# One core, a hybrid state-space and attention trunk: state-space tensors regrouped by chunk through DRAM, softmax tiles copied per query tile, one Gelu

## The chip, the cores and the metric

One NeuronCore of a Trainium2 chip runs the whole program. The metric is device time in microseconds (us) of one execution. The engines are TensorE (PE in the rows, with PEld for its weight loads), VectorE (DVE), ScalarE (ACT), GpSimd (POOL) and SyncE (SP), which here issues nearly every DMA, from one queue and in a fixed order.

## The reference, cut to what matters

One layer, sequence of 512 positions, model width 2048, everything in float32.

```
proj = h @ w_in            # u | conv | q k v | indexer
# (A) S5 state space, 512 channels in 32 groups of 16, then Gelu and a GLU
y = Re(C x) + d * u,  x[t] = lam_bar * x[t-1] + B_bar u[t]
g = gelu(y);  y_ssm = g * sigmoid(g @ w_glu + b_glu)
# (B) gated short convolution
# (C) 8 heads of 128: keys chosen by an indexer (top-k), then
s = softmax(q k^T * scale, masked to the chosen keys);  y_attn = s v
y = concat(rms(y_ssm), rms(y_conv), rms(y_attn)) @ w_o     # then LayerNorm
out = LayerNorm(alpha * x + gate * (relu(h2 @ w_ff1)^2 @ w_ff2))
```

## The kernel before, in words

One function, `trunk_kernel`, is written with a tile framework. Each engine runs one static list of instructions; the framework sets that list from the order of the code and from priorities (`with prio("ssm")`: each block has an offset in a table). Blocks of higher priority run where their data allow; the large float32 matmuls of the projections, which are split in two halves each (`wh`, `wl`), fill the rest of TensorE. Tensors lie transposed, channels on the partitions.

The program runs in stages. From 0 to about 235 us come the conditioning vector and the first input projections, among them `u_t` (128 x 4 x 512: the 512 state-space channels over time). From about 235 to 445 us come the rotary embedding of q and k (`cos_t`, `sin_t`, L401 to L419, with `sw` as its scratch tile), the indexer and the top-k, which are VectorE work, over the projection of k on TensorE. From about 440 to 710 us the projections of v (`wv`, evacuated from PSUM by ACT copies into `ve`) and of the convolution (`wconv`) fill TensorE, and the state space and the attention are woven into them. Then come the GLU, the output projection (`wo`), LayerNorm and the two feed-forward products, up to the end.

The state space goes in four rounds m of 128 channels. `ssm_in` (L674) loads `bc`, builds small matrices on DVE, and regroups `u_t[:, m]` from channels x time into `uc`, in which a partition holds one of four places in a chunk and 32 channels: 16 ACT copies of 32 x 128 elements. `ssm_scan` (L711) multiplies (L716) and runs the recurrence on DVE. `ssm_direct` (L736) prepares the matrices of the direct part. `ssm_out` (L773) does the output matmuls (L777 to L779) into a PSUM bank (`sb`), copies them back to channels x time with another 16 ACT copies of 32 x 128, into a tile that is also called `uc`, adds `d * u` on DVE and applies Gelu on ACT. The GLU (L800) loads its weights `wg` and multiplies (L807).

The attention goes by head h and query tile t. `att_scores` (L858): one score matmul (L863) into one of two PSUM banks named `sa`, mask and minimum on DVE (L866), exponential on ACT, reciprocal on DVE, scaling on ACT (`s`). `att_turn` (L873): t+1 transposes (L876) into an `sa` bank, and t+1 ACT copies of 128 x 128 into the tiles `pt0` to `pt3`, one for each tile of keys. `att_values` (L880): four matmuls (L884), 512, 384, 256 and 128 columns wide, into an `sa` bank, an ACT copy into `qh`, and a write to `y_d`. Both banks of `sa` are shared by scores, transposes and values, so a late ACT copy out of one holds the next of them.

Every ACT copy goes through a helper and has the line L57; most DVE operations have L60 or L63.

Of the kernel before, what the change touches and what calls it, by code (L numbers as in the profile page):

```python
# [51 lines left out]
def trunk_kernel(ctx, tc, A, out):  # L52
    nc = tc.nc
    V, S, G, T = nc.vector, nc.scalar, nc.gpsimd, nc.tensor

    def act(o, i, f=AF.Copy, **kw):
        S.activation(o, i, f, **kw)  # L57
# [4 lines left out]
    def stt(o, a, s, b, op0, op1):  # L62
        V.scalar_tensor_tensor(o, a, s, b, op0=op0, op1=op1)  # L63
# [17 lines left out]
    def prio(name):  # L81
        if name not in PRIO:
            name += str(stage_no[0])
        return tc.high_priority(offset=PRIO[name])
# [14 lines left out]
    def col(n, i=0, w=1):  # L99
        o = COLS[n][0]  # L100
        return cols[:, o + i:o + i + w]
# [306 lines left out]
    nc.sync.dma_start(cos_t, A["rope_q"][0])  # L408
    nc.sync.dma_start(sin_t, A["rope_q"][1])

    def rope_t(dst, src):

        sw = TB.tile([128, SEQ], F32, name="sw", bufs=2)
        act(sw[0:64], src[64:128])
        act(sw[64:128], src[0:64])
        tt(dst, src, cos_t, OP.mult)
        tt(sw, sw, sin_t, OP.mult)
        tt(dst, dst, sw, OP.add)
# [257 lines left out]
    def ssm_in(m):  # L676

        p4 = slice(4 * m, 4 * m + 4)

        def pb(x, s):  # L680
            return x[:, p4, 0:s, None].to_broadcast([128, 4, s, 16])

        bc = SP.tile([128, 4, 4, 16], F32, name="bc")
        nc.sync.dma_start(bc, A["ssm_bc"][:, :, p4])
        uc = SP.tile([128, 4, 128], F32, name="uc", bufs=2)
        uv = u_t[:, m].rearrange("p (c s) -> p s c", s=4)
        for s in range(4):
            for p in range(4):
                act(uc[32 * s:32 * s + 32, p], uv[32 * p:32 * p + 32, s])
        tmp = SP.tile([128, 2, 4, 5, 16], F32, name="tmp")  # L690
        bb = SP.tile([128, 2, 4, 16], F32, name="bb")
        f_b = tuple(f[:, p4, None].to_broadcast([128, 4, 16]) for f in (fr, fi))
        cmul((bb[:, 0], bb[:, 1]), f_b, (bc[:, 0], bc[:, 1]), (tmp[:, 0, :, 0], tmp[:, 1, :, 0]))
        bt = SP.tile([128, 2, 4, 128], F32, name="s4", bufs=2)
        G.memset(bt, 0.0)
        ta, tb_ = tmp[:, 0, :, 0:4], tmp[:, 1, :, 0:4]
        tt(ta, pb(pwr[:, 0], 4), vb(bb[:, 0], 4), OP.mult)
        tt(tb_, pb(pwr[:, 1], 4), vb(bb[:, 1], 4), OP.mult)
        outer(bt[:, 0], ta, tb_, 4, OP.subtract)
        tt(ta, pb(pwr[:, 0], 4), vb(bb[:, 1], 4), OP.mult)  # L700
        tt(tb_, pb(pwr[:, 1], 4), vb(bb[:, 0], 4), OP.mult)
        outer(bt[:, 1], ta, tb_, 4, OP.add)
        bl = SP.tile([128, 2, 4, 128], F32, name="s4", bufs=2)
        for ri in range(2):
            ps = bank("sb")
            for p in range(4):
                T.transpose(ps[:, p * 128:(p + 1) * 128], bt[:, ri, p], ident)
            act(bl[:, ri].rearrange("p a b -> p (a b)"), ps)
        return p4, bc, bb, bl, uc
# [63 lines left out]
    def ssm_out(m, uc, x):  # L773
        ps = bank("sb")
        for p in range(4):
            o = ps[:, p * 128:(p + 1) * 128]
            T.matmul(o, toep[:, p], uc[:, p], start=True, stop=False)  # L777
            T.matmul(o[:, 1:128], cl[:, 0, p, 32:160], x[:, 0, p, 0:127], start=False, stop=False)
            T.matmul(o[:, 1:128], cl[:, 1, p, 32:160], x[:, 1, p, 0:127], start=False, stop=True)  # L779
        yt = SP.tile([128, SEQ], F32, name="uc", bufs=2)  # L780
        yv = yt.rearrange("p (c s) -> p s c", s=4)
        for t in range(4):
            for p in range(4):
                act(yv[32 * p:32 * p + 32, t], ps[32 * t:32 * t + 32, p * 128:(p + 1) * 128])
        stt(u_t[:, m], u_t[:, m], col("d", m), yt, OP.mult, OP.add)
        act(u_t[:, m], u_t[:, m], AF.Gelu_apprx_tanh)

    with prio("ssm"):
        s_in = ssm_in(0)
        for m in range(4):  # L790
            x = ssm_scan(*s_in)
            p4, bc, bb, bl, uc = s_in
            ssm_direct(p4, bc, bb)
            if m < 3:
                s_in = ssm_in(m + 1)
            ssm_out(m, uc, x)
    ssm.close()
    glu = ExitStack()
    GL = glu.enter_context(tc.tile_pool(name="glu", bufs=1, reuse_waits="tile", side="right"))
    with prio("glu"):  # L800
        wg = GL.tile([128, 4, 512], F32, name="wg")
        nc.sync.dma_start(wg, A["wglu"])
        sig = GL.tile([128, 4, SEQ], F32, name="sig")
        for m in range(4):
            ps = bank("sb")
            for k in range(4):
                T.matmul(ps, wg[:, k, m * 128:(m + 1) * 128], u_t[:, k], start=(k == 0), stop=(k == 3))  # L807
            act(sig[:, m], ps, AF.Sigmoid, bias=col("bglu", m))
        for m in range(4):
            tt(u_t[:, m], u_t[:, m], sig[:, m], OP.mult)  # L810

        ps = rms_rows(GL, square_sum(GL, [u_t[:, m] for m in range(4)], (1, 1)), 512, "sb")
        for m in range(4):
            stt(u_t[:, m], u_t[:, m], col("gn", m), ps, OP.mult, OP.mult)

# [31 lines left out]
    def att_load(h):  # L849
        qh = AT.tile([128, SEQ], F32, name="qh", bufs=2)  # L850
        kh = AT.tile([128, SEQ], F32, name="kh")
        vh = AT.tile([128, NT, 128], F32, name="vh")
        nc.sync.dma_start(qh, q_d[h])
        nc.sync.dma_start(kh, k_d[h])
        nc.sync.dma_start(vh, v_d[:, :, h * 128:(h + 1) * 128].rearrange("t p n -> p t n"))
        heads[h] = qh, kh, vh, [AT.tile([128, SEQ - 128 * j], F32, name=f"pt{j}") for j in range(NT)]

    def att_scores(h, t):  # L858

# [12 lines left out]
    def att_turn(h, t, s):  # L872

        pb_ = bank("sa")
        for j in range(t + 1):
            T.transpose(pb_[:, j * 128:(j + 1) * 128], s[:, j * 128:(j + 1) * 128], ident)  # L876
        for j in range(t + 1):
            act(heads[h][3][j][:, (t - j) * 128:(t - j + 1) * 128], pb_[:, j * 128:(j + 1) * 128])

    def att_values(h):  # L880
        qh, _, vh, pt = heads.pop(h)
        po = bank("sa")
        for j in range(NT):
            T.matmul(po[:, j * 128:], vh[:, j], pt[j], start=(j == 0), stop=(j == NT - 1))  # L884
        act(qh, po)
        nc.sync.dma_start(y_d[h], qh)
        if h == 0:
            act(sqa, qh, AF.Square)
        else:
            sq = AT.tile([128, SEQ], F32, name="s", bufs=3)  # L890
            act(sq, qh, AF.Square)
            tt(sqa, sqa, sq, OP.add)
# [14 lines left out]
        att_turn(*last)  # L907
        att_values(NH - 1)

    rsa = AT.tile([128, SEQ], F32, name="rsa")  # L910
    act(rsa, rms_rows(AT, sqa, 1024, "sa"))


# [700 lines left out]
```

## Time and profile before

| | |
|---|---|
| time, median of 3 runs | 2243.91 us (2243.41 to 2245.91) |
| the profiled execution | 2243.67 us, of which its span is 2241.9 us |
| instructions | 30919 |
| PE busy | 2151.6 us, 96% of the span |
| DVE busy | 1880.8 us, 84% |
| ACT busy | 1096.3 us, 49% |
| mean granted TensorE clock | 0.985 |

The profiled execution is one run on the chip with the hardware profiler; its span is from its first instruction to its last. Shares of busy time are means over stages that have different limits, so the rows further down are taken by stage. PE busy counts matmul time alone; weight loads (PEld) run beside it.

### The profile page before, as it was taken

What the parts mean: (1) busy time and instruction counts of PE and PEld (TensorE: products, weight loads), DVE (VectorE), ACT (ScalarE), POOL (GpSimd) and SP (SyncE); (2) the same over time, 40 slices, a digit from 0 to 9 for tenths busy, and PEclk for the clock granted to TensorE, in tenths of its full rate; (3) what the DMA queues carried; (4) which work ended last, traced back from release to release, by engine and by line L of the source; (5) the groups of instructions that cost most, each with busy time, mean ns of one, the idle gap of its engine ahead of it and who ended that gap; (6) DMA issues with size and microseconds to landing.
All of it is one profiled execution on the core that took longest, in us unless ns stands there. A gap on an engine that the chain in (4) does not pass through costs nothing.

```text
span 2241.9 us, 30919 instructions
## 1 busy us (share of the span) xinstructions
PE 2151.6 (96%) x11947; PEld 1848.8 (82%) x11947; DVE 1880.8 (84%) x2520; ACT 1096.3 (49%) x1570; POOL 44.6 (2%) x55
## 2 busy tenths in 40 slices
PE   6999999988899999999999999999899999999997
PEld 4778887866676787889999999999778888888886
DVE  7886889998776777698888888887689989998788
ACT  3322444467864312656656566665444444444432
POOL 0000000000000000000000000000000000000000
PEclk9999999999999999999999999999999999999999
DMA  8877554254314577656656656565788898798462
GB/s 323 320 296 275 187 196 153 104 205 138 102 66 155 197 281 285 208 191 208 208 188 203 209 181 207 179 206 166 264 284 264 313 324 267 257 347 273 129 220 85
DMA packets 192411, 485.60 MB, mean 217 GB/s; under 512 B 17412, under 2 KB 101764, under 8 KB 165896
## 3 DMA queue, kind: packets, MB, share of 16 engines
q1 hardware_dynamic: 185736, 471.04, 59.3%
q0 software_dynamic: 6528, 12.58, 3.1%
q8 instruction: 94, 1.54, 0.3%
q14 instruction: 53, 0.43, 0.1%
HBM read 392.35 MB, written 78.64 MB: 210 GB/s over the span
## 4 chain that ended last, share of the span: by engine, by line
PE 68%; DVE 20%; ACT 5%; DMA 4%; issue 3%; SPq 0%; DVEq 0%; ACTq 0%
PE mm L203 8%; PE mm L204 7%; PE mm L202 7%; PE two L1380 5%; PE two L1381 5%; PE two L1379 5%; DVE wl L60 5%; PE mm L197 4%; PE mm L198 3%; PE mm L196 3%; PE mm L210 3%; PE mm L209 3%; PE mm L208 3%; DVE ffa L60 2%; DVE adaz L63 2%
## 5 line engine op out<-in xcount | busy, mean ns | idle before, releaser
L57 ACT ACTIVATE wh<-raw 128x1024 fp32r<-128x1024 f32 x332 | 351.3, 1059 | 446.9 <-PE two L1381 141.5
L60 DVE TENSOR_TENSOR wl<-raw,wh 128x1024 fp32r<-128x1024 f32 x332 | 403.5, 1219 | 108.2 <-ACT wh L57 107.3
L1379 PE MATMUL two<-wh,hin 128*128 128x512 f32 x784 | 307.6, 392 | 5.8 <-ACT wh L57 5.1
L1380 PE MATMUL two<-wl,hin 128*128 128x512 f32 x784 | 306.4, 391 | 2.3 <-DVE wl L60 2.3
L1381 PE MATMUL two<-wh,hin 128*128 128x512 f32 x784 | 306.1, 390 | 0.0
L196 PE MATMUL mm<-acts,wh 128*128 128x512 f32 (+1 forms) x568 | 226.9, 403 | 7.2 <-ACT ve L57 3.8
L197 PE MATMUL mm<-acts,wl 128*128 128x512 f32 (+1 forms) x568 | 225.9, 398 | 0.8 <-DVE wl L60 0.7
L198 PE MATMUL mm<-acts,wh 128*128 128x512 f32 (+1 forms) x568 | 224.6, 396 | 0.0
L63 DVE SCALAR_TENSOR_TENSOR adaz<-raw,cols,adaz 128x1024 f32<-128x1024 f32 (+2 forms) x180 | 198.1, 1111 | 16.2 <-DMA raw<-in_adaR_dram 10.9
L202 PE MATMUL mm<-acts,wh 128*128 128x256 f32 x720 | 204.7, 284 | 3.5 <-ACT wh L57 2.4
L203 PE MATMUL mm<-acts,wl 128*128 128x256 f32 x720 | 204.5, 284 | 1.7 <-DVE wl L60 1.7
L203 PE MATMUL mm<-tx,wl 128*128 128x256 f32 x720 | 203.8, 283 | 1.1 <-DVE wl L60 1.1
L204 PE MATMUL mm<-acts,wh 128*128 128x256 f32 x720 | 204.4, 284 | 0.0
L204 PE MATMUL mm<-tx,wh 128*128 128x256 f32 x720 | 203.4, 282 | 0.0
L202 PE MATMUL mm<-tx,wh 128*128 128x256 f32 x720 | 202.0, 281 | 0.1
L1379 PEld LDWEIGHTS two<-wh,hin 128*128 128x128 f32 x784 | 147.8, 189 | 38.3 <-ACT wh L57 6.3
L1380 PEld LDWEIGHTS two<-wl,hin 128*128 128x128 f32 x784 | 147.8, 188 | 35.1 <-DVE wl L60 4.0
L209 PE MATMUL mm<-wl,acts 128*128 128x512 f32 x448 | 175.0, 391 | 1.2 <-DVE wl L60 1.0
L210 PE MATMUL mm<-wh,acts 128*128 128x512 f32 x448 | 174.7, 390 | 0.0
L208 PE MATMUL mm<-wh,acts 128*128 128x512 f32 x448 | 173.7, 391 | 0.2 <-DVE r L60 0.2
L1381 PEld LDWEIGHTS two<-wh,hin 128*128 128x128 f32 x784 | 147.6, 188 | 30.9
L57 ACT ACTIVATE wh<-st 128x1024 fp32r<-128x1024 f32 x90 | 95.4, 1060 | 105.5 <-PE mm L204 83.9
(316 smaller groups left out, 4581.1 us busy)
## 6 DMA issues: line engine op xcount, KB each, us to landing
raw<-in_wff_dram SPq DMA_DIRECT2D x232, 512.0 KB, 4.6
hc_d<-hc SPq DMA_DIRECT2D x98, 512.0 KB, 5.0
hin<-hc_d SPq DMA_DIRECT2D x49, 1024.0 KB, 8.6
raw<-in_adaR_dram SPq DMA_DIRECT2D x48, 1024.0 KB, 5.2
raw<-in_adaS_dram SPq DMA_DIRECT2D x32, 1024.0 KB, 8.7
raw<-in_wo_dram SPq DMA_DIRECT2D x16, 1024.0 KB, 5.1
araw<-in_adaR_dram SPq DMA_DIRECT2D x16, 1024.0 KB, 7.7
raw<-in_wconv_dram SPq DMA_DIRECT2D x12, 1024.0 KB, 4.8
```

The costliest lines, as they stand in the source:

```text
L57: S.activation(o, i, f, **kw)
L60: V.tensor_tensor(o, a, b, op=op)
L63: V.scalar_tensor_tensor(o, a, s, b, op0=op0, op1=op1)
L196: T.matmul(ps, wh, xh, start=start, stop=False)
L197: T.matmul(ps, wl, xh, start=False, stop=False)
L198: T.matmul(ps, wh, xl, start=False, stop=stop)
L202: T.matmul(ps, wh, xh, start=start, stop=False, skip_group_check=True)
L203: T.matmul(ps, wl, xh, start=False, stop=False, skip_group_check=True)
L204: T.matmul(ps, wh, xl, start=False, stop=stop, skip_group_check=True)
L1379: T.matmul(ps[:, t], xh, h[:, k], start=first, stop=False, skip_group_check=True)
L1380: T.matmul(ps[:, t], xh, l[:, k], start=False, stop=False, skip_group_check=True)
L1381: T.matmul(ps[:, t], xl, h[:, k], start=False, stop=last, skip_group_check=True)
```

## The change

It has six parts.

1. At the start of the rotary stage, four ACT copies (128 x 512, into `us`, in the buffers of `sw`) regroup `u_t` by place in the chunk, and 16 DMAs of 64 KB, issued by SP, write them to a DRAM tensor `u_d`. `ssm_in` then loads `uc` by one DMA of 256 KB and has no ACT copies.
2. `ssm_out` takes its PSUM bank with one ACT copy of 128 x 512 (`yo`), writes it to `yc_d` with four DMAs of 64 KB and reads it back with one of 256 KB (`yt`); the addition on DVE goes over a strided view of `u_t`. `uc` has three buffers in place of two.
3. Gelu runs once, over all four tiles (128 x 2048), after the last round.
4. In the GLU `sig` is allocated ahead of `wg`, and a small tile `pad` is added.
5. The turned softmax tiles are kept by query tile: `att_turn` makes one ACT copy of 128 to 512 columns, and `att_values` makes ten matmuls of 128 columns in place of four wider ones, over the same number of columns.
6. `rsa` takes the buffer of `kh`.

```diff
--- before.py
+++ after.py
@@ -407,6 +407,21 @@
     sin_t = TB.tile([128, SEQ], F32, name="sin_t")
     nc.sync.dma_start(cos_t, A["rope_q"][0])
     nc.sync.dma_start(sin_t, A["rope_q"][1])
+
+    u_d = dram.tile([4, 128, 4, 128], F32, name="u_d")
+    yc_d = dram.tile([4, 128, 4, 128], F32, name="yc_d")
+
+    def by_place(x):
+        return x.rearrange("p (c s) -> p s c", s=4)
+
+    with prio("rope"):
+        for m in range(4):
+            us = TB.tile([128, 4, 128], F32, name="sw", bufs=2)
+            act(us, by_place(u_t[:, m]))
+            for p in range(4):
+                nc.sync.dma_start(u_d[m].rearrange("(s r) p c -> p r s c", s=4)[p], us[32 * p:32 * p + 32])
 
     def rope_t(dst, src):
 
@@ -682,11 +697,8 @@
 
         bc = SP.tile([128, 4, 4, 16], F32, name="bc")
         nc.sync.dma_start(bc, A["ssm_bc"][:, :, p4])
-        uc = SP.tile([128, 4, 128], F32, name="uc", bufs=2)
-        uv = u_t[:, m].rearrange("p (c s) -> p s c", s=4)
-        for s in range(4):
-            for p in range(4):
-                act(uc[32 * s:32 * s + 32, p], uv[32 * p:32 * p + 32, s])
+        uc = SP.tile([128, 4, 128], F32, name="uc", bufs=3)
+        nc.sync.dma_start(uc, u_d[m])
         tmp = SP.tile([128, 2, 4, 5, 16], F32, name="tmp")
         bb = SP.tile([128, 2, 4, 16], F32, name="bb")
         f_b = tuple(f[:, p4, None].to_broadcast([128, 4, 16]) for f in (fr, fi))
@@ -777,13 +789,13 @@
             T.matmul(o, toep[:, p], uc[:, p], start=True, stop=False)
             T.matmul(o[:, 1:128], cl[:, 0, p, 32:160], x[:, 0, p, 0:127], start=False, stop=False)
             T.matmul(o[:, 1:128], cl[:, 1, p, 32:160], x[:, 1, p, 0:127], start=False, stop=True)
-        yt = SP.tile([128, SEQ], F32, name="uc", bufs=2)
-        yv = yt.rearrange("p (c s) -> p s c", s=4)
+        yo = SP.tile([128, 4, 128], F32, name="uc", bufs=3)
+        act(yo.rearrange("p a b -> p (a b)"), ps)
         for t in range(4):
-            for p in range(4):
-                act(yv[32 * p:32 * p + 32, t], ps[32 * t:32 * t + 32, p * 128:(p + 1) * 128])
-        stt(u_t[:, m], u_t[:, m], col("d", m), yt, OP.mult, OP.add)
-        act(u_t[:, m], u_t[:, m], AF.Gelu_apprx_tanh)
+            nc.sync.dma_start(yc_d[m].rearrange("(p r) t c -> t r p c", p=4)[t], yo[32 * t:32 * t + 32])
+        yt = SP.tile([128, 4, 128], F32, name="uc", bufs=3)
+        nc.sync.dma_start(yt, yc_d[m])
+        stt(by_place(u_t[:, m]), by_place(u_t[:, m]), col("d", m), yt, OP.mult, OP.add)
 
     with prio("ssm"):
         s_in = ssm_in(0)
@@ -794,13 +806,14 @@
             if m < 3:
                 s_in = ssm_in(m + 1)
             ssm_out(m, uc, x)
+        act(u_t, u_t, AF.Gelu_apprx_tanh)
     ssm.close()
     glu = ExitStack()
     GL = glu.enter_context(tc.tile_pool(name="glu", bufs=1, reuse_waits="tile", side="right"))
     with prio("glu"):
+        sig = GL.tile([128, 4, SEQ], F32, name="sig")
         wg = GL.tile([128, 4, 512], F32, name="wg")
         nc.sync.dma_start(wg, A["wglu"])
-        sig = GL.tile([128, 4, SEQ], F32, name="sig")
         for m in range(4):
             ps = bank("sb")
             for k in range(4):
@@ -812,6 +825,8 @@
         ps = rms_rows(GL, square_sum(GL, [u_t[:, m] for m in range(4)], (1, 1)), 512, "sb")
         for m in range(4):
             stt(u_t[:, m], u_t[:, m], col("gn", m), ps, OP.mult, OP.mult)
+
+        GL.tile([128, 136], F32, name="pad")
 
@@ -853,7 +868,7 @@
         nc.sync.dma_start(qh, q_d[h])
         nc.sync.dma_start(kh, k_d[h])
         nc.sync.dma_start(vh, v_d[:, :, h * 128:(h + 1) * 128].rearrange("t p n -> p t n"))
-        heads[h] = qh, kh, vh, [AT.tile([128, SEQ - 128 * j], F32, name=f"pt{j}") for j in range(NT)]
+        heads[h] = qh, kh, vh, [AT.tile([128, 128 * t + 128], F32, name=f"pt{t}") for t in range(NT)]
 
     def att_scores(h, t):
 
@@ -874,14 +889,15 @@
         pb_ = bank("sa")
         for j in range(t + 1):
             T.transpose(pb_[:, j * 128:(j + 1) * 128], s[:, j * 128:(j + 1) * 128], ident)
-        for j in range(t + 1):
-            act(heads[h][3][j][:, (t - j) * 128:(t - j + 1) * 128], pb_[:, j * 128:(j + 1) * 128])
+        act(heads[h][3][t], pb_[:, 0:(t + 1) * 128])
 
     def att_values(h):
         qh, _, vh, pt = heads.pop(h)
         po = bank("sa")
-        for j in range(NT):
-            T.matmul(po[:, j * 128:], vh[:, j], pt[j], start=(j == 0), stop=(j == NT - 1))
+        for t in range(NT):
+            for j in range(t + 1):
+                T.matmul(po[:, t * 128:(t + 1) * 128], vh[:, j], pt[t][:, j * 128:(j + 1) * 128],
+                         start=(j == 0), stop=(j == t))
         act(qh, po)
         nc.sync.dma_start(y_d[h], qh)
         if h == 0:
@@ -907,7 +923,7 @@
         att_turn(*last)
         att_values(NH - 1)
 
-    rsa = AT.tile([128, SEQ], F32, name="rsa")
+    rsa = AT.tile([128, SEQ], F32, name="kh")
     act(rsa, rms_rows(AT, sqa, 1024, "sa"))
 
```

The order of instructions shifts with it. First, ACT where the first half of the v projection leaves PSUM: `wh<-raw` are halves of weights, `uc<-u_t` the regrouping copies of the state space, `prm` small state-space parameters, `ve<-mm` the evacuations of the v projection. Before:

```order
L57 ACTIVATE wh<-raw 128x1024 x5
L57 ACTIVATE uc<-u_t 32x128 x5
L57 ACTIVATE wh<-raw 128x1024
L57 ACTIVATE uc<-u_t 32x128 x22
L57 ACTIVATE wh<-raw 128x1024
L57 ACTIVATE uc<-u_t 32x128
L57 ACT_TABLE_LOAD
L57 ACTIVATE prm<-prm 128x16
L57 ACTIVATE uc<-u_t 32x128 x4
L57 ACTIVATE prm<-prm 128x16
L57 ACTIVATE ve<-mm 128x512 x3
```

After:

```order
L57 ACTIVATE ve<-mm 128x512
L57 ACTIVATE wh<-raw 128x1024 x7
L57 ACTIVATE ve<-mm 128x512
L57 ACT_TABLE_LOAD
L57 ACTIVATE prm<-prm 128x16 x2
L57 ACTIVATE ve<-mm 128x512 x2
L57 ACTIVATE wh<-raw 128x1024
L57 ACTIVATE ve<-mm 128x512
```

The 32 copies `uc<-u_t` of rounds 0 and 1 stood ahead of the last three evacuations and stand nowhere in this stretch now.

Second, ACT at the state-space output of a middle round, in the midst of the attention: `pt` are copies of turned softmax tiles (the number is that of a buffer), `sa` and `sb` the PSUM banks of attention and state space, `s` softmax tiles, `s,st` an exponential with its sum. Before:

```order
L57 ACTIVATE pt_4822<-sa 128x128
L57 ACTIVATE pt_4823<-sa 128x128
L57 ACTIVATE pt_4824<-sa 128x128
L57 ACTIVATE uc<-sb 32x128 x14
L57 ACTIVATE qh<-sa 128x512
L57 ACTIVATE uc<-sb 32x128
L57 ACTIVATE s<-qh 128x512
L57 ACTIVATE s,st<-s,st 128x256
L57 ACTIVATE uc<-sb 32x128
L57 ACTIVATE pt_4897<-sa 128x128
L57 ACTIVATE s<-s,st 128x256
L57 ACT_TABLE_LOAD
```

After:

```order
L57 ACTIVATE s,st<-s,st 128x512
L57 ACTIVATE s<-s,st 128x512
L57 ACTIVATE uc<-sb 128x512
L57 ACTIVATE pt_4900<-sa 128x384
L57 ACTIVATE s,st<-s,st 128x128
L57 ACTIVATE x<-sb 128x512
L57 ACTIVATE s<-s,st 128x128
L57 ACTIVATE pt_4901<-sa 128x512
L57 ACTIVATE x<-sb 128x512
L57 ACTIVATE qh<-sa 128x512
L57 ACTIVATE s<-qh 128x512
```

Sixteen copies `uc<-sb` became one, the four `pt` copies of 128 columns became one of 512, and a table load fell out between them. Over the whole order the table loads of ACT go from 12 to 7.

Third, the queue of SP at the start of the rotary stage: `raw` are weights, `cni` and `sni` the indexer's tables. Before:

```order
L127 DMA raw<-in_wk_dram 128x2048
L408 DMA cos_t<-in_rope_q_dram 128x512
L409 DMA sin_t<-in_rope_q_dram 128x512
L428 DMA cni<-in_rope_i_dram 128x192
L429 DMA sni<-in_rope_i_dram 128x192
```

After:

```order
L127 DMA raw<-in_wk_dram 128x2048
L408 DMA cos_t<-in_rope_q_dram 128x512
L424 DMA u_d<-sw 32x4x128 x13
L127 DMA raw<-in_adaR_dram 128x2048
L424 DMA u_d<-sw 32x4x128 x3
L409 DMA sin_t<-in_rope_q_dram 128x512
L443 DMA cni<-in_rope_i_dram 128x192
L444 DMA sni<-in_rope_i_dram 128x192
```

All 16 writes of `u_d` and one load of weights stand between `cos_t` and `sin_t`.

## Rows read from the trace of the kernel before

**Rows 1.** The page, part 1: busy us of each engine, share of the span, instructions.

```profile
PE 2151.6 (96%) x11947; PEld 1848.8 (82%) x11947; DVE 1880.8 (84%) x2520; ACT 1096.3 (49%) x1570; POOL 44.6 (2%) x55
```

**Rows 2.** Windows (us): sum, PE, PEld, DVE, ACT, POOL busy (instructions), granted clock, DMA share, GB/s.

```profile
400.00:450.00 50.00, 50.00 (x221) 41.05 (x220) 48.90 (x103) 21.93 (x37) 3.08 (x6) 1.00 0.31 108
450.00:500.00 50.00, 43.92 (x205) 33.98 (x204) 45.99 (x168) 29.83 (x65) 3.12 (x7) 0.93 0.62 218
500.00:550.00 50.00, 43.52 (x211) 32.97 (x211) 40.83 (x113) 36.56 (x90) 1.91 (x2) 0.97 0.42 133
550.00:600.00 50.00, 41.36 (x204) 29.96 (x202) 36.44 (x114) 42.83 (x109) 1.14 (x2) 0.97 0.34 108
600.00:650.00 50.00, 41.69 (x196) 31.36 (x195) 33.11 (x97) 42.47 (x109) 1.72 (x2) 0.90 0.26 92
650.00:700.00 50.00, 46.07 (x217) 36.05 (x216) 40.36 (x78) 22.07 (x40) 0.95 (x1) 0.97 0.32 121
700.00:750.00 50.00, 49.70 (x206) 36.25 (x205) 37.55 (x51) 22.00 (x36) 0.00 (x0) 1.00 0.39 137
```

**Rows 3.** Waits of PE from 420 to 830 us: who waits, releaser: us, times, longest.

```profile
PE sa L876 <- ACT qh L57: 8.1, 3, 3.3
PE sb L716 <- ACT uc L57: 6.6, 3, 3.4
PE sa L876 <- ACT s L57: 4.0, 4, 1.9
PE mm L196 <- ACT ve L57: 3.8, 1, 3.8
PE sb L807 <- DMA wg<-in_wglu_dram: 2.7, 1, 2.7
```

**Rows 4.** Timeline, ACT and PE: start us, us, instruction [idle before <- releaser].

```profile
533.22 4.81 ACT L57 ACTIVATE uc<-sb 32x128 f32<-32x128 f32 x12
538.08 1.16 PE L716 MATMUL sb<-uc,s 128*128 128x128 f32 x8 [3.36 <-ACT uc L57]
582.37 5.62 ACT L57 ACTIVATE uc<-sb 32x128 f32<-32x128 f32 x14 [1.40 <-PE sb L779]
588.01 0.60 ACT L57 ACTIVATE qh<-sa 128x512 f32<-128x512 f32 x1
588.67 0.33 PE L876 MATMUL sa<-ident,s 128*128 128x128 f32 x1 [3.27 <-ACT qh L57]
```

**Rows 5.** Groups of ACT by form, 440 to 740 us: busy us, mean ns | idle before.

```profile
L57 ACT ACTIVATE uc<-u_t 32x128 f32<-32x128 f32 x64 | 27.5, 429 | 0.8
L57 ACT ACTIVATE uc<-sb 32x128 f32<-32x128 f32 x64 | 24.9, 389 | 5.6 <-PE sb L779 4.8
L57 ACT ACTIVATE pt<-sa 128x128 f32<-128x128 f32 x80 | 17.2, 276 | 2.0 <-PE sa L876 1.8
L57 ACT ACT_TABLE_LOAD x11 | 14.1, 1283 | 0.2
```

**Rows 6.** The chain that ended last, around 599 us: start, us, instruction.

```profile
598.80 0.89 PE sb L716 x8
```

**Rows 7.** Timeline of PE, the value matmuls of one head.

```profile
602.18 2.42 PE L884 MATMUL sa<-pt,vh 128*128 128x512 f32 x8
```

**Rows 8.** Groups by line, 190 to 830 us: weight loads of the value matmuls.

```profile
L884 PEld LDWEIGHTS sa<-pt,vh 128*128 128x128 f32 x64 | 11.6, 190 | 9.0 <-ACT pt L57 3.9 <-issue 2.4
```

**Rows 9.** DMA issues, 190 to 760 us: KB each, median us to landing.

```profile
kh<-k_d SPq DMA_DIRECT2D x8, 256.0 KB, 2.6
y_d<-qh SPq DMA_DIRECT2D x8, 256.0 KB, 2.6
```

**Rows 10.** Timeline of SP: DMA issues (start, us).

```profile
232.98 0.43 SPq L409 DMA_DIRECT2D sin_t<-in_rope_q_dram  x1
690.34 0.33 SPq L802 DMA_DIRECT2D wg<-in_wglu_dram  x1
```

**Rows 11.** Timeline of DVE: first use of the sine table.

```profile
239.29 0.68 DVE L60 TENSOR_TENSOR sw<-sw,sin_t 128x512 f32<-128x512 f32 x1
```

## The prediction, as put on record before the changed kernel ran

> **What bounds the kernel now.** I read the shares of busy time first. TensorE is busy 96% of the span and ACT 49% [rows 1], so over the whole program nothing that ACT saves is worth anything unless TensorE waits for it somewhere. The second view, the windows, says where that is. Up to 450 us and again from 700 us TensorE is busy 49.7 to 50 us of every 50; between them it stands idle for 6.1 + 6.5 + 8.6 + 8.3 + 3.9 = 33.4 us, and the clock granted falls below 1 in each of these five windows [rows 2]. That is just the stretch of state space and attention which the change rewrites. After it TensorE is saturated to the end with the same work in the same order, so each us won there comes off the end.
>
> The third view, the waits of TensorE in that stretch, says for whom it waits: 8.1 us for the copy `qh`, 6.6 for `uc`, 4.0 for `s`, 3.8 for `ve`, all ACT's, and 2.7 for the DMA of `wg` [rows 3]. Together 25.2 us, three quarters of the idle time. The fourth, the timeline, shows that the operation named is not always the cause. At 582.37 ACT begins 14 small `uc` copies, 5.62 us; only then does `qh` run, 0.60 us, and the transposes that need the bank which `qh` frees had by then waited 3.27 us. At 533.22 twelve such copies hold up L716 for 3.36 us [rows 4]. ACT is not short of time there (22 to 43 us of 50 [rows 2]); it is late, because blocks of small copies stand ahead of what TensorE needs next.
>
> **What the change takes off ACT.** From 440 to 740 us the 64 copies `uc<-u_t` take 27.5 us and the 64 copies `uc<-sb` 24.9 [rows 5]. The first move to four copies in an earlier stage, and the second become four of 128 x 512, at the 0.60 us of `qh` [rows 4] 2.4 us. Five table loads fewer at 1.283 us are 6.4 us. Of the `pt` copies 48 of 80 go; 128 columns take 276 ns and 512 take 600, which puts what does not grow with width near 168 ns, so 48 of them are 8.1 us. That makes 64 us less of ACT's 174 from 450 to 700.
>
> **What this is worth, wait by wait.** `uc` (6.6): the copies are gone, all of it. `ve` (3.8): 32 `uc` copies stood ahead of the last three evacuations and are gone; all. `wg` (2.7): its load was issued at 690.34 [rows 10], since its buffer lay where the last output was read; with `sig` there instead it can be issued earlier; all. `qh` (8.1): what stood ahead of it is gone or one copy; I keep a tenth, so 7.3. `s` (4.0): half of it is the chain of DVE and ACT itself, which stays; 2.0. Sum 22.4 us.
>
> **The clock.** The windows from 450 to 700 lose 0.07 + 0.03 + 0.03 + 0.10 + 0.03 of 50 us each [rows 2]: 13 us of TensorE at full speed, if it had work all that time, and 11 at its busy share of 87%. Each of these windows has idle TensorE in it, and those without idle time have 1.00. What comes back when two thirds of the idle time goes cannot be read from before; the bounds are 0 and 11, and I take 4, toward the lower end because some idle time stays.
>
> **Value matmuls.** A head's pass over the same columns goes from 8 instructions, 2.42 us [rows 7], to 20 of 128 columns. Eight of 128 took 0.89 us in one place [rows 6] and 1.16 in another [rows 4], so 20 take 2.2 to 2.9: over eight heads -1.6 to +3.9 us. I take 0, as the cheaper one is nearer to matmuls that wait for nothing. Twelve weight loads more per head at 190 ns [rows 8] are 18.2 us if nothing covers them. In 0.89 us eight matmuls with eight loads fit, 111 ns each, less than one such load, so loads run beside matmuls there; I take 0 and keep 18 as a rival. The Trainium skill ("TensorE: Matmul & The Clock Gate", section "LDWEIGHTS (loading the stationary operand)") gives a load the number of its columns over 1.2 in ns, 107 for 128; that is under the 190 of the row, which holds waiting too. By that figure uncovered loads would be an estimated 10 us, and the time about 2233.
>
> **The sine table.** `sin_t`, issued at 232.98 now and used at 239.29 [rows 10, 11], comes behind 16 writes and one load of weights. 17 issues at 0.43 us are 7.3 us, and with two buffers the third and fourth copies wait for writes to land, twice about 0.6 + 2.6 [rows 9]: some 13.7 us later. DVE's rotary work is held by that, and DVE has 1.1 us of 50 to spare up to 450 [rows 2]. What DVE loses may come out at the start of attention: 0 to 13.7 us. I take 2, because TensorE has projections to run until 450 and attention waited for ACT.
>
> **The trips through DRAM.** An output now writes `yc_d` and reads it back before DVE can add: 2.6 us each [rows 9] and five issues at 0.43, 7.4 us with nothing beside it. What it replaces, 16 copies at 389 ns [rows 5], was 6.2 us in the same place of the chain, so the chain grows by some 2 us with the one copy. What is queued behind on SP are loads of `kh`, `vh` and weights. Bounds 0 and 4 x 7.4 = 29.4; I take 3, because before the GLU nothing on TensorE reads the output. The Trainium skill speaks against this part ("DMA: Bandwidth & Descriptors", section "Anatomy of one DMA — SWDGE (gpsimd) path"): a fixed cost of about 2.0 us whatever the size. By that a trip is an estimated 4.7 us, four of them 19 us if all show; the 2.6 of the row for 256 KB agrees with it, and no row shows a write of 64 KB.
>
> One Gelu, the strided addition and `rsa` I count at nothing: DVE and ACT have room while the convolution's matmuls run (37.6 and 22.0 of 50 after 700 [rows 2]); without that cover one Gelu of 2048 columns is some 2 us ahead of the GLU.
>
> **Sum.** On the profiled execution's 2243.67 us, 0.24 under the median: -22.4 - 4 + 0 + 2 + 3 = -21.4, which gives 2222.3 us. About 4.5 us, 0.2%, is what can be told from no change.
>
> **Rivals.** (a) *DVE becomes the bound.* State-space work moves forward, and DVE has only 4.0 us of 50 to spare from 450 to 500 and 9.2 to 550 [rows 2]. If it paces that stretch, the 12.6 us of idle TensorE in it stay: 2235. For it: 92% busy. Against it: no wait of TensorE on DVE is among the five largest [rows 3]. (b) *The late sine table* shows in full: 11.7 more than I took, 2234. (c) *Weight loads are not covered*: 18.2 more, 2240.5; against it stands 0.89 us. (d) *The change does not do what it says*: TensorE waits for `s`, behind the same chain of scores, instead of for `uc` and `qh`; only `ve` and `wg` fall, -6.5 + 2 + 3: 2242. (e) *The SP queue makes it slower*: SP issues in order, and a DMA that waits for a copy or a write to land holds those behind it, `kh` and `vh` of the next head among them. If each of four outputs shows its 7.4 us, 29.4 takes the place of 3 and the clock gives nothing back: 2243.7 - 22.4 + 2 + 29.4 = 2252.7. It decides from 6.3 us an output on. Against it: 6.2 us of copies leave the same place. (f) *More than forecast*: all 25.2 us of waits and 11 of clock: 2206 to 2213.
>
> **How the numbers follow.** My forecast, 2213 to 2232, has a chance of 0.55; (f) 0.06, (a) 0.13, (b) 0.06, (c) 0.03, (d) 0.06, (e) 0.11. The first four are faster by over 0.2% (below 2239.4): 0.80. (c) and (d) are the same: 0.09. (e) is slower: 0.11. The range from 2208 to 2241 holds the forecast, (a), (b) and (c) and most of (f), about 0.81, and leaves out (e), part of (d) and the end of (f).
>
> **What would show it.** In the trace after, right: no `uc` copies in blocks on ACT; waits of L716 on `uc` and of L876 on `qh` under 1 us in sum; windows from 450 to 700 with under 15 us of idle TensorE; `wg` issued before the last output. Wrong: waits on the DMA of `uc` or `kh` in their place (e); DVE at 48 of 50 from 450 on with TensorE waiting behind it (a); a gap on DVE at 240 to 255 ahead of the product with `sin_t` (b); 20 value matmuls above 3 us (c). The forecast fails most easily where what follows the small copies was late anyway, for the chain of a head's softmax is as long as before but for the copies.

## The result and the profile after

The changed kernel takes 2222.24 us, median of four runs (2218.12 to 2224.48), beside 2243.68 for the kernel before on the same chip (2243.41 to 2245.91): a ratio of 0.9899, 95% interval 0.9877 to 0.9921. That is 21.4 us less, with 2222.3 forecast. The profiled execution is the fastest of the four, 2218.12 us with a span of 2216.3; its mean granted clock is 0.993, that of the other three 0.990 to 0.991. So what this profile shows as won, 25.6 us, is 4 us more than the median.

The page, part 1, as [rows 1]:

```profile
PE 2138.7 (96%) x12043; PEld 1845.9 (83%) x12043; DVE 1878.6 (85%) x2520; ACT 1041.5 (47%) x1394; POOL 44.6 (2%) x55
```

PE's busy time fell by 12.9 us and its idle time, span less busy, from 90.3 to 77.6 us, by 12.7. Ten value matmuls now do the work of four, so nothing in the change takes work off TensorE; what did change is the clock granted to it. ACT saves 55 us. The windows of the stretch that the change rewrites, columns as in [rows 2]:

```profile
450.00:500.00 50.00, 46.66 (x239) 36.37 (x238) 48.38 (x183) 26.31 (x54) 3.12 (x7) 1.00 0.68 240
500.00:550.00 50.00, 43.43 (x242) 34.59 (x241) 47.14 (x124) 26.07 (x56) 1.90 (x2) 0.99 0.48 161
550.00:600.00 50.00, 46.49 (x267) 36.09 (x266) 46.79 (x149) 32.02 (x74) 2.87 (x3) 0.98 0.38 119
600.00:650.00 50.00, 45.52 (x266) 37.59 (x266) 39.29 (x97) 26.76 (x52) 0.95 (x1) 0.97 0.33 106
650.00:700.00 50.00, 49.94 (x198) 35.38 (x198) 29.48 (x39) 24.09 (x34) 0.00 (x0) 1.00 0.39 132
```

From 450 to 700 us TensorE is idle for 18.0 us where it was 33.4, and the granted clock, 0.06 short in the sum of the five windows where it was 0.26, loses 3 us of 250 instead of 13. DVE is busy 47 to 48 of 50 us up to 600. The five longest waits of TensorE from 420 to 830 us, and the one for `qh`, as [rows 3]:

```profile
PE sa L891 <- ACT s L57: 4.9, 8, 2.6
PE sb L719 <- DVE s L60: 3.8, 4, 2.6
PE mm L196 <- ACT ve L57: 2.3, 2, 1.2
PE sa L543 <- DVE sqa L60: 2.2, 1, 2.2
PE sa L899 <- DVE st L881: 1.4, 2, 1.1
...
PE sa L891 <- ACT qh L57: 0.8, 2, 0.4
```

The waits for `uc` and `wg` are gone, that for `qh` is a tenth of what it was, and `ve` has 2.3 us of its 3.8 left. No wait for a DMA stands among them. All waits of TensorE for DVE that this view lists, short ones included, grew from 4.4 us to 9.9. ACT's groups by form, 440 to 740 us, answering to [rows 5]:

```profile
L57 ACT ACT_TABLE_LOAD x6 | 7.7, 1283 | 5.9 <-DMA raw<-in_adaR_dram 5.8
...
L57 ACT ACTIVATE pt<-sa 128x512 f32<-128x512 f32 x8 | 4.7, 591 | 5.5 <-PE sa L891 5.5
L57 ACT ACTIVATE pt<-sa 128x384 f32<-128x384 f32 x8 | 3.8, 480 | 0.6 <-PE sa L891 0.6
L57 ACT ACTIVATE pt<-sa 128x256 f32<-128x256 f32 x8 | 3.0, 372 | 1.2 <-PE sa L891 1.2
L57 ACT ACTIVATE uc<-sb 128x512 f32<-128x512 f32 x4 | 2.4, 598 | 3.2 <-PE sb L791 3.2
L57 ACT ACTIVATE pt<-sa 128x128 f32<-128x128 f32 x8 | 2.1, 264 | 0.0
```

The 52.4 us of `uc` copies are 2.4 here, beside four copies into `us` before this stretch, 1.12 us each, and the table loads fell by 6.4. The `pt` copies saved only 3.6 us (17.2 to 13.6), not the 8.1 estimated: the 80 copies before, at 276 ns each, would be 22.1 us one after the other, but kept ACT busy for 17.2, since copies in a row overlap in the trace.

Last, the trip of the third output through DRAM, in SP's timeline, and the DMA groups of the change (KB each, median us to landing), beside [rows 9]:

```profile
605.32 1.77 SPq L795 DMA_DIRECT2D yc_d<-uc  x4
610.39 0.38 SPq L870 DMA_DIRECT2D vh<-v_d  x1
610.94 0.38 SPq L797 DMA_DIRECT2D uc<-yc_d  x1
611.41 0.38 SPq L902 DMA_DIRECT2D y_d<-qh  x1
```

```profile
u_d<-sw SPq DMA_DIRECT2D x16, 64.0 KB, 1.8
uc<-u_d SPq DMA_DIRECT2D x4, 256.0 KB, 5.2
...
yc_d<-uc SPq DMA_DIRECT2D x16, 64.0 KB, 1.8
uc<-yc_d SPq DMA_DIRECT2D x4, 256.0 KB, 4.7
```

The 5.2 and 4.7 are medians, that of `uc<-u_d` from the one landing that the trace has. The read of this third output landed in 3.2 us, so from the first issue at 605.32 to its landing, 610.94 + 3.2, are 8.8 us. The small writes land in 1.8; the read stands in the queue behind `vh`, whose issue waits 3.2 us for value matmuls, and then takes longer than the 2.6 of the loads of `kh`, which are of the same size. The four trips, counted in this way, take 10.7, 7.3, 8.8 and 9.0 us, with reads of 5.3, 4.1, 3.2 and 5.4.

### The profile page after: what moved, and what is told of

Its sections match the earlier page's. It is cut to its first block, busy times and chain, and to the rows that moved or that the text cites. A ratio compares the mean times of both kernels' runs of the same rounds, so it can differ in the third digit from the quotient of the medians.

```text
span 2216.3 us, 30985 instructions
## 1 busy us (share of the span) xinstructions
PE 2138.7 (96%) x12043; PEld 1845.9 (83%) x12043; DVE 1878.6 (85%) x2520; ACT 1041.5 (47%) x1394; POOL 44.6 (2%) x55
## 4 chain that ended last, share of the span: by engine, by line
PE 50%; issue 29%; DVE 14%; DMA 4%; ACT 3%; SPq 0%; POOL 0%; DVEq 0%; ACTq 0%; POOLq 0%
PE two L1396 7%; PE two L1397 7%; PE two L1395 7%; PE mm L209 4%; PE mm L197 4%; PE mm L210 4%; PE mm L208 3%; PE mm L198 3%; PE mm L196 3%; DVE wl L60 3%; DVE adaz L63 2%; PE two L210 1%; PE two L209 1%; PE two L208 1%; DVE x L60 1%
## 5 line engine op out<-in xcount | busy, mean ns | idle before, releaser
L196 PE MATMUL mm<-acts,wh 128*128 128x512 f32 (+1 forms) x568 | 223.0, 396 | 5.7 <-ACT wh L57 3.3
L198 PE MATMUL mm<-acts,wh 128*128 128x512 f32 (+1 forms) x568 | 221.2, 391 | 0.0
L63 DVE SCALAR_TENSOR_TENSOR adaz<-raw,cols,adaz 128x1024 f32<-128x1024 f32 (+2 forms) x180 | 198.2, 1111 | 16.9 <-DMA raw<-in_adaR_dram 12.8
```

What stands on the lines that cost most here:

```text
L196: T.matmul(ps, wh, xh, start=start, stop=False)
L198: T.matmul(ps, wh, xl, start=False, stop=stop)
```

## The experiments

The theory: small ACT copies stood, as blocks, ahead of what TensorE needed; moving both regroupings to DMAs ends these waits and what the clock lost in the same windows, and the other parts of the change are worth next to nothing. Rivals: the gain is in the other parts; the trips through DRAM or the late sine table cost what they bring; DVE, now 95% busy, is the next limit. Ratios are to the kernel before on the same chip. The runs were on several chips, on which the kernel before took 2241.26 to 2246.25 us, so kernels are compared by ratio; 0.1% is 2.2 us.

| kernel | median us | ratio, 95% interval | idle PE 450 to 700 us | PE idle, span | PE busy |
|---|---|---|---|---|---|
| before (first chip) | 2243.68 | 1 | 33.4 | 90.3 | 2151.6 |
| changed | 2222.24 | 0.9899 (0.9877 to 0.9921) | 18.0 | 77.6 | 2138.7 |
| inputs by ACT again | 2233.83 | 0.9976 (0.9963 to 0.9988) | 24.3 | 86.4 | 2147.2 |
| outputs by ACT again | 2237.56 | 0.9985 (0.9972 to 0.9998) | 26.6 | 91.6 | 2148.7 |
| `pt` by keys again | 2223.87 | 0.9921 (0.9905 to 0.9936) | 17.8 | 79.0 | 2143.9 |
| `wg` first again | 2224.95 | 0.9925 (0.9908 to 0.9943) | 17.4 | 77.0 | 2141.1 |
| Gelu per tile again | 2221.70 | 0.9893 (0.9875 to 0.9910) | 17.5 | 75.2 | 2144.6 |
| both, regroupings only | 2221.05 | 0.9895 (0.9876 to 0.9914) | 16.6 | 74.5 | 2140.9 |
| sine table first | 2223.92 | 0.9905 (0.9888 to 0.9922) | 18.0 | 79.6 | 2140.9 |
| changed, less DVE | 2223.28 | 0.9906 (0.9888 to 0.9924) | 17.9 | 80.9 | 2139.1 |
| before, less DVE | 2239.51 | 0.9984 (0.9974 to 0.9994) | 32.5 | 92.8 | 2144.4 |

The last three columns are from the profiled execution of each: window and span less PE busy time, and PE busy time. That of the changed kernel is 4 us below its median, that of the outputs by ACT 4.5 above.

**Inputs by ACT again.**

```diff
-        nc.sync.dma_start(uc, u_d[m])
+        uv = u_t[:, m].rearrange("p (c s) -> p s c", s=4)
+        for s in range(4):
+            for p in range(4):
+                act(uc[32 * s:32 * s + 32, p], uv[32 * p:32 * p + 32, s])
```

The four copies of `u_t` into `us` and the writes of `u_d` are left out too.

> The changed kernel (2222.2 us) with the inputs of the state space regrouped by 64 small ACT copies again, and without the tensor u_d; all else as changed. By the prediction's terms the 32 copies stand ahead of the evacuations ve again (3.8 us), one wait of the scan's matmuls on uc comes back (up to 3.4), sine table and SP queue are as before (-2), and some half clock returns: 2226 to 2234, most likely 2230. Rival, that the relief of ACT was not what paid here because DVE is the next limit anyway: within 4 us of 2222. Rival, that the early copies and the late sine table cost as much as they bring: under 2220.

Measured 2233.83, at the upper end of the theory's span; by ratio it stands for 2238 on the first chip, 4 us past it. The timeline of ACT and PE in this kernel shows two of the waits that were taken away:

```profile
444.52 9.65 ACT L57 ACTIVATE uc<-u_t 32x128 f32<-32x128 f32 x22
...
459.76 0.79 PE L196 MATMUL mm<-acts,wh 128*128 128x512 f32 x1 [3.81 <-ACT ve L57]
...
593.07 3.06 ACT L57 ACTIVATE uc<-u_t 32x128 f32<-32x128 f32 x7
596.15 0.60 ACT L57 ACTIVATE qh<-sa 128x512 f32<-128x512 f32 x1
...
596.80 0.47 PE L887 MATMUL sa<-ident,s 128*128 128x128 f32 x1 [3.28 <-ACT qh L57]
```

The 22 copies ahead of `ve` cost TensorE 3.81 us, as before the change, and the seven ahead of `qh` 3.28; no wait on `uc`, which was expected too, is in this kernel.

The late `ve` does more than that. Its writes to `v_d`, and behind them in SP's queue the loads of the first heads, go out later (the first of these loads at 471.38, at 472.38 before, at 461.73 in the changed kernel), and attention starts later. The first score matmuls in the kernel before, the changed one, this one and the next:

```profile
480.34 0.89 PE L863 MATMUL sa<-kh,qh 128*128 128x128 f32 x4 [1.34 <-DMA kh<-k_d]
467.57 0.89 PE L878 MATMUL sa<-kh,qh 128*128 128x128 f32 x4
479.80 1.50 PE L874 MATMUL sa<-kh,qh 128*128 128x128 f32 x4 [1.98 <-DMA kh<-k_d]
468.85 0.89 PE L877 MATMUL sa<-kh,qh 128*128 128x128 f32 x4
```

With the inputs by DMA attention starts 11 to 13 us earlier, with them by ACT as late as before. The prediction has no term for this.

**Outputs by ACT again.**

```diff
-        yo = SP.tile([128, 4, 128], F32, name="uc", bufs=3)
-        act(yo.rearrange("p a b -> p (a b)"), ps)
+        yt = SP.tile([128, SEQ], F32, name="uc", bufs=3)
+        yv = yt.rearrange("p (c s) -> p s c", s=4)
         for t in range(4):
-            nc.sync.dma_start(yc_d[m].rearrange("(p r) t c -> t r p c", p=4)[t], yo[32 * t:32 * t + 32])
-        yt = SP.tile([128, 4, 128], F32, name="uc", bufs=3)
-        nc.sync.dma_start(yt, yc_d[m])
-        stt(by_place(u_t[:, m]), by_place(u_t[:, m]), col("d", m), yt, OP.mult, OP.add)
+            for p in range(4):
+                act(yv[32 * p:32 * p + 32, t], ps[32 * t:32 * t + 32, p * 128:(p + 1) * 128])
+        stt(u_t[:, m], u_t[:, m], col("d", m), yt, OP.mult, OP.add)
```

> The changed kernel with the outputs of the state space regrouped by 64 small ACT copies again, no trip through yc_d; all else as changed. By the prediction's terms blocks of 16 copies (some 6 us) stand ahead of qh and uc once more: of the 8.1 us for qh and the waits on uc about 7 to 10 us come back, with some half clock: 2228 to 2236, most likely 2231. Rival, that the trip through DRAM costs about what the copies cost: within 4 us of 2222. Rival, that the trip is the dearer: under 2219.

Measured 2237.56, 1.6 us past the span given, and 4 past it by ratio: nearly the whole gain is lost. A block of this kernel, ACT and PE, and its longest wait:

```profile
577.08 6.41 ACT L57 ACTIVATE uc<-sb 32x128 f32<-32x128 f32 x16 [1.39 <-PE sb L791]
583.51 0.60 ACT L57 ACTIVATE qh<-sa 128x512 f32<-128x512 f32 x1
...
583.54 1.16 PE L728 MATMUL sb<-uc,s 128*128 128x128 f32 x8 [3.60 <-ACT uc L57]
```

```profile
PE sb L728 <- ACT uc L57: 10.7, 3, 3.6
```

L728 starts when the block ends, 0.05 us behind it, though its own operand `uc` comes by DMA in this kernel. What is left for it to wait for is the bank that the 16 copies empty: the pool `sb` has one buffer, and L728 writes it next. So a block does two things: it holds a PSUM bank for 6.4 us in place of 0.6, and it delays what stands behind it on ACT, here `qh`. Only the first cost TensorE much in this kernel: its waits for `qh` are 0.3 us in all, not the several us that were expected back.

Each regrouping put back by itself costs 0.8 to 0.9% of the time, together 1.6, and the whole change brought 1.0. The parts are not to be added: either sort of block alone keeps most of the loss. The clock is part of it. The stretch from 450 to 700 us before, with the inputs and with the outputs by ACT (the clock is the third figure from the end; the changed kernel has 0.99):

```profile
450.00:700.00 250.00, 216.56 (x1025) 164.31 (x1024) 196.72 (x567) 173.75 (x409) 8.85 (x13) 0.95 0.39 135
450.00:700.00 250.00, 225.69 (x1157) 175.79 (x1156) 198.37 (x573) 148.61 (x304) 8.84 (x13) 0.96 0.42 143
450.00:700.00 250.00, 223.41 (x1152) 172.15 (x1151) 199.79 (x576) 151.20 (x318) 8.83 (x13) 0.97 0.39 134
```

Against the changed kernel TensorE's busy time over the whole span is 8.5 us longer with the inputs by ACT and 10.0 with the outputs, beside 8.8 and 14.0 us more idle time; some of that is the chance of the executions that were profiled.

**The other parts.** First the softmax tiles, with the copies and value matmuls of the kernel before:

```diff
-        heads[h] = qh, kh, vh, [AT.tile([128, 128 * t + 128], F32, name=f"pt{t}") for t in range(NT)]
+        heads[h] = qh, kh, vh, [AT.tile([128, SEQ - 128 * j], F32, name=f"pt{j}") for j in range(NT)]
...
-        act(heads[h][3][t], pb_[:, 0:(t + 1) * 128])
+        for j in range(t + 1):
+            act(heads[h][3][j][:, (t - j) * 128:(t - j + 1) * 128], pb_[:, j * 128:(j + 1) * 128])
...
-        for t in range(NT):
-            for j in range(t + 1):
-                T.matmul(po[:, t * 128:(t + 1) * 128], vh[:, j], pt[t][:, j * 128:(j + 1) * 128],
-                         start=(j == 0), stop=(j == t))
+        for j in range(NT):
+            T.matmul(po[:, j * 128:], vh[:, j], pt[j], start=(j == 0), stop=(j == NT - 1))
```

> The changed kernel with the turned softmax tiles by tile of keys again: 80 copies of 128 columns, four value matmuls a head. The prediction counts nothing for the matmuls, and 8 us less of ACT only where TensorE waits for it: 2221 to 2226. Rival, that the copies after a transpose are on the chain of a head (the last four of them 1.1 us where one takes 0.6): 2227 or more. Rival, that 96 weight loads more cost time in the changed kernel: under 2219.

Next the two lines in the GLU:

```diff
-        sig = GL.tile([128, 4, SEQ], F32, name="sig")
         wg = GL.tile([128, 4, 512], F32, name="wg")
         nc.sync.dma_start(wg, A["wglu"])
+        sig = GL.tile([128, 4, SEQ], F32, name="sig")
```

> The changed kernel with wg allocated ahead of sig again, so that its load waits for what lay there. By the prediction's term 2.7 us come back: 2224 to 2227. Rival: the load of wg is not what the first GLU matmul waits for in the changed kernel, within 1.5 us of 2222.

Then Gelu inside the loop:

```diff
         stt(by_place(u_t[:, m]), by_place(u_t[:, m]), col("d", m), yt, OP.mult, OP.add)
+        act(u_t[:, m], u_t[:, m], AF.Gelu_apprx_tanh)
...
-        act(u_t, u_t, AF.Gelu_apprx_tanh)
```

> The changed kernel with Gelu once for each of the four tiles again, behind each output, which brings its table loads of 1.28 us back among the exponentials of the softmax. The prediction counts nothing for one Gelu as such, and 6.4 us of ACT in table loads only where TensorE waits: 2222 to 2225. Rival, that the four exchanges of tables lie on the chain of the softmax: 2227 or more. Rival, that one Gelu late is the dearer, since the GLU waits for all of it: under 2220.

And the softmax tiles and Gelu put back at once, which leaves the two regroupings, with their buffers, the order of `sig` and `wg`, `pad`, and `rsa` in the buffer of `kh`:

> The changed kernel with softmax tiles by tile of keys and Gelu once per tile as before the change; the two regroupings through DRAM (with the three buffers of uc, and sig ahead of wg) stay. Either of these two put back alone gave 2221.7 and 2223.9. If the whole gain is that of the two regroupings together, 2220 to 2228. Rival, that the parts stand in for each other, so that with both put back ACT blocks TensorE again: 2232 or more.

Measured 2223.87, 2224.95, 2221.70 and 2221.05. All four intervals overlap that of the changed kernel, and idle TensorE from 450 to 700 us is 16.6 to 17.8 us in each. Without the softmax copies and the single Gelu the two regroupings make the whole gain (0.9895 for 0.9899). By ratio `pt` by keys and `wg` first, each by itself, are 0.2 to 0.3% slower than the changed kernel, some 5 us, with intervals that just overlap: these times neither show nor exclude that they cost something. For `pt` the last kernel speaks against it. For `wg` the trace does: that the order of `wg` and `sig` ended its wait can be excluded, since in the kernel with the old order the load is issued at 652.36, behind the last output, and TensorE has no wait for it either; it still has other matmuls until the load lands, 4.8 us later.

**The sine table first.**

```diff
-    nc.sync.dma_start(cos_t, A["rope_q"][0])
-    nc.sync.dma_start(sin_t, A["rope_q"][1])
+    with prio("rope"):
+        nc.sync.dma_start(cos_t, A["rope_q"][0])
+        nc.sync.dma_start(sin_t, A["rope_q"][1])
```

> The changed kernel with the loads of cosine and sine table at the priority of the writes of u_d, so that both are issued ahead of these. The prediction counted 2 us for the late sine table: 2219 to 2222. Rival, that its whole delay of some 14 us is lost: 2208 to 2213. Rival, that it costs nothing, since DVE catches up before attention begins: within 1 us of 2222.

Measured 2223.92: nothing to tell from the changed kernel. The first product with the table, in DVE's timeline of the changed kernel and of this one (at 239.29 before [rows 11]):

```profile
254.87 0.69 DVE L60 TENSOR_TENSOR sw<-sw,sin_t 128x512 f32<-128x512 f32 x1 [0.32 <-DMA sin_t<-in_rope_q_dram]
```

```profile
251.49 0.69 DVE L60 TENSOR_TENSOR sw<-sw,sin_t 128x512 f32<-128x512 f32 x1
```

It came 15.6 us later, of which the table's place in the queue made 3.4, and winning these back brought nothing. The other 12.2 us no run isolates; late as the rotary embedding is, the first score matmul comes 12.8 us earlier than before (467.57 for 480.34).

**Is DVE the next limit?** First, conditioning products moved off the stretch:

```diff
-PUMP = dict(start=0, keys=2, values=0, conv=1, wo=1.5)
+PUMP = dict(start=0, keys=2, values=0, conv=0, wo=2)
```

> The changed kernel with one number changed: no conditioning products (DVE, 128 x 1024, 1.28 us each, 15 of them from 450 to 640 us) while the convolution is projected; they come in the output projection instead. After the change DVE is busy 47 to 48 of 50 us from 450 to 600 and stands in the chain there. If DVE's time is what is short now, 19 us of it freed give 4 to 10 us: 2212 to 2218. Rival, that the length of the chain of a head sets the pace and DVE's load does not matter: within 3 us of 2222. Rival, that the products are missed in the output projection: 2225 or more.

The same in the kernel before:

> The kernel before the change with the same number changed. If ACT's blocks of small copies were the limit before, freeing DVE brings little there: 0 to 3 us less than before (2241 to 2244). Rival, that DVE limited the stretch before too: the same 4 to 10 us as in the changed kernel.

Measured 2254.83 (ratio 1.0044, 1.0027 to 1.0061) and 2282.60 (1.0163, 1.0141 to 1.0184). Both have a new wait, here the changed kernel's timeline:

```profile
781.54 2.05 PE L246 MATMUL sc<-adaz,ones 128*128 128x512 f32 x2 [23.70 <-DVE adaz L63]
```

The products come too late in the output projection and TensorE stands 23.7 us, so the times of these two say nothing on DVE before 700 us. The trace of the changed kernel with this edit does: from 450 to 700 us DVE is busy 192.5 us for 211.1, and TensorE idle 19.6 for 18.0. The next pair takes work away for good: the last step of the recurrence is left out. These are 16 products and 16 sums, not 32 of each as the first expectation below says: 18.9 us at 0.59 us each, and 15.5 us less of DVE's busy time in the changed kernel, since they overlap in the trace.

```diff
-        for ri in range(2):
-            dst = xv[:, ri, :, 1:16, 0:7]
-            for cc in range(2):
-                w = SP.tile([128, 4, 15, 7], F32, name="w")
...
-                tt(dst, dst, w, OP.subtract if (ri, cc) == (0, 1) else OP.add)
```

> The changed kernel without the last step of the recurrence (the carry into the 15 later blocks of a row: 32 products and 32 sums on DVE, 0.59 us each, 18.9 us in all, of which 4.7 us in each round's chain); the outputs of the state space are not those of the reference. If DVE is the next limit between 450 and 640 us, 6 to 14 us less: 2208 to 2216. Rival, that what is left are waits of the softmax chain on ACT and PSUM: within 4 us of 2222.

> The kernel before the change without the same step of the recurrence, 18.9 us of DVE. If ACT's blocks of small copies set the pace there, little comes of it: 2238 to 2244. Rival, that DVE set the pace before as well: 6 to 14 us less, 2230 to 2238.

Measured 2223.28 and 2239.51. The stretch from 450 to 700 us in the changed kernel, and in the same kernel with less work for DVE:

```profile
450.00:700.00 250.00, 232.05 (x1206) 180.03 (x1205) 211.08 (x585) 135.25 (x268) 8.85 (x13) 0.99 0.45 151
```

```profile
450.00:700.00 250.00, 232.09 (x1214) 180.97 (x1213) 197.50 (x554) 135.20 (x268) 8.82 (x13) 0.99 0.46 155
```

DVE has 13.6 us less to do there and TensorE is as busy as before, within 0.04 us. DVE's share of busy time, 95% up to 600 us, is not the limit. That DVE holds nothing up does not follow: TensorE's longest waits in this run are those for DVE's `s`, which were 3.8 us in the changed kernel:

```profile
PE sb L719 <- DVE s L60: 6.7, 5, 2.7
```

In the kernel before, the same edit brought 0.16%, with 32.5 us of idle time in the stretch for 33.4.

Last, 16 operations from DVE to the idle GpSimd (`G`, which `outer` now takes as its engine):

```diff
-        outer(cl[:, 0], ta, tb_, 5, OP.subtract)
+        outer(cl[:, 0], ta, tb_, 5, OP.subtract, G)
...
-        outer(cl[:, 1], ta, tb_, 5, OP.add)
+        outer(cl[:, 1], ta, tb_, 5, OP.add, G)
```

> The changed kernel with the 16 last operations on cl (64 x 320, 0.485 us each on DVE, 7.8 us in all) on GpSimd, which is idle there; the results are the same. If DVE's time is short from 450 to 600 us: 2216 to 2221. Rival, that GpSimd takes so long for them that the matmuls of the direct part are late: 2224 or more. Rival, that DVE's time is not short: within 1.5 us of 2222.

Measured 2230.27 (ratio 0.9937, 0.9922 to 0.9952), slower than the changed kernel. GpSimd's group (440 to 740 us), a wait of DVE and one of TensorE:

```profile
L689 POOL TENSOR_TENSOR cl<-tmp 64x320 f32<-64x320 f32 x16 | 15.3, 956 | 46.0 <-PE sb L793 41.2 <-DVE tmp L60 2.1 <-DVE st L886 2.1
```

```profile
DVE tmp L60 <- POOL cl L689: 6.0, 4, 2.0
```

```profile
PE sb L722 <- DVE s L60: 8.1, 5, 4.2
```

One of them takes 956 ns for DVE's 485. The Trainium skill ("GPSIMD Engine Reference", section "4.1 Engine selection") gives GpSimd about twice DVE's time for operations of two inputs, and these runs agree, at 1.97. And DVE waits 6.0 us until `tmp`, of which there is one buffer, is read. TensorE's waits for DVE's next matrices `s` are then 8.1 us for 3.8. So this run shows what the move costs, not what DVE's time is worth.

## Why the prediction was right, point by point

**What bounds the kernel: right.** TensorE's waits on late ACT copies between 450 and 700 us were the place, and what was won there came off the end. The two experiments that put copies back brought the waits back with them. But that TensorE is busy 49.7 to 50 of every 50 us elsewhere holds only for the two windows of [rows 2] beside the stretch: 56.9 of its 90.3 us of idle time lay outside it, and 59.6 of 77.6 do after the change. And attention starts earlier, which was not forecast; that is likely a part of the gain, but no run isolates it from the waits.

**Wait by wait: too large by a third.** The sum of idle time was to fall by 22.4 - 5 = 17.4 us; in the profiled execution it fell by 12.7, by 15.4 in the stretch. The five waits named fell by 17.2 of their 25.2 us, where 22.4 was forecast, and waits for DVE took back 5.5. `uc` (6.6) went wholly and `qh` by 7.3, as forecast. `ve` was counted whole at 3.8 and gave 1.5; `s` was counted at half of 4.0 and grew to 4.9; and 3.8 us of waiting for DVE's `s` at L719, 1.1 before, came in. `wg` (2.7) went, but not for the reason given: its load is issued at 649.88, behind the last output and not ahead of it, and the old order of the two tiles shows no wait either. Two signs named for being right thus failed, `wg` ahead of the last output and under 15 us of idle TensorE in the stretch (18.0). The price of the `pt` copies was wrong as well, 8.1 us for 3.6, but the sum did not use it.

**The clock: the term that was mis-sized.** I took 4 of 0 to 11 us. The windows from 450 to 700 give 10, and PE's busy time over the whole span fell by 12.9, or 14.3 with the 1.4 us that value matmuls grew by. Some of that is chance: the runs of one kernel differ by 6 us with a mean clock between 0.990 and 0.993, and this profile is the best of them; and from 0 to 200 us, where both kernels do the same work, the windows lose 3.5 us to the clock in this profile and 7 in that of the kernel before. At the median, 21.4 less the 12.7 of idle time leaves an estimated 9 us for it, twice the 4. So the forecast met the median to 0.1 us because idle time brought less and the clock more, and that the two errors cancel is luck.

**Value matmuls, weight loads: right.** Value matmuls went from 19.0 to 20.4 us busy in all, inside the bounds of -1.6 to +3.9. The 160 weight loads are busy 19.0 us beside them, with 1.4 us of waits of the matmuls, on DVE; 18 us uncovered did not come.

**Sine table, trips through DRAM: covered.** I counted 2 and 3 us. The rotary work on DVE came 15.6 us later and cost nothing that putting the table first could win back. Three of the four trips take 8.8 to 10.7 us, more than the 7.4 that I gave as the upper bound, since the read queues behind other loads on SP and lands in 3.2 to 5.4 us. Rival (e) would have needed that time to show; no wait of TensorE names it. Covered as it is, the trip pays: with the copies in its place the time is 0.9% longer. The rule cited for it, the Trainium skill ("DMA: Bandwidth & Descriptors", section "Anatomy of one DMA — SWDGE (gpsimd) path"), with its fixed cost of about 2.0 us, is stated for DMAs that GpSimd issues, and SP issues these. It is near the 1.8 us of the 64 KB writes; the reads of `uc`, at 3.2 to 5.4 us, are above the 2.6 that it gives for 256 KB. Long or short, the trip was hidden, so what the rule spoke against did not come.

**DVE becomes the bound, rival (a): the sign was there, the limit was not.** DVE went to 47 and 48 of 50 us and stands behind 9.9 us of waits of TensorE, but 13.6 us less of it in the stretch won nothing. Which chain holds the 18 us of idle time that are left was not settled: freeing DVE left it, and removing waits on ACT's `s` alone was not tried.

Rivals (b), (c) and (f) did not come; of (d), the part came that waits for `s` did not shrink. Why either kind of block put back alone loses nearly all of the gain is shown only in part: the named waits came back (3.8 and 3.3 us; 10.7 us), the clock fell with them, attention started late with the inputs, and with these there were also 3.5 us of waits for DVE's `x` (1.8 before, none in the changed kernel), so that the order around them counts as well.

## What to carry to other kernels

Where a saturated engine waits for an engine that is half idle, look for blocks of many small operations in the queue of the second: each block delays what stands behind it, and holds the buffer that it empties, by its whole length. Moving such a regrouping to DMAs paid here even though the trip takes longer than the copies, because nothing on the busy engine waits for it; check that, and not the trip's time. Look also at what the late copies hold up further on, in DMA queues above all: here it was the start of the next stage. A busy share of 95% beside a waiting engine is no proof of a limit: take work away and see, and leave out what merely moves it to where it will be waited for.

## What was not expected of the hardware

A read of 256 KB from DRAM landed in 2.6 us for `kh` (the median) and in 3.2 to 5.4 us for `uc`, of the same size and from tensors that the kernel had written. The two slowest read-backs, 5.3 and 5.4 us, were issued 0.6 and 0.5 us behind a load of 1 MB, the fastest, 3.2, behind one of 256 KB, so what is in flight ahead of a read is the likely cause; no run isolates it. Strided views took longer than was priced: the four ACT copies of 128 x 512 that regroup `u_t` take 1.12 us each, where the unstrided copy `s<-qh` takes 0.63, and the addition on DVE over a strided view takes 1.15 us for 0.75. Four runs of one program on one chip spread over 6 us, with mean clocks from 0.990 to 0.993, which is as much as most single parts of this change could have brought.
